# A hybrid decoder block on one core: sliding keys and latents projected ahead of the lower top-k searches, and a power seed for the reciprocal roots

## The chip, the cores and the metric

The kernel runs on one core of a Trainium2 chip. The metric is the device time of one execution in microseconds (us); times of stretches and instructions come from one profiled execution of the kernel before. The engines are named as the profile names them: PE (TensorE, matrix products, with its weight loads as PEld), DVE (VectorE), ACT (ScalarE), POOL (GpSimd) and SP (SyncE, which here only issues DMAs). Each engine works through its own queue of instructions in order.

## The reference

The program computes one layer of a decoder over 1024 tokens of width 1024, with 16 learned meta tokens ahead of them:

```
hn = rms_norm(h)                                  # h: 16 meta + 1024 tokens
aq, ak, av, bq, bkv, iq, ik, iw, gates = split(hn @ w_in)
o_a = sliding_window_attention(aq, ak, av)        # 8 heads, 2 key heads, window 128, sinks, bias
q_abs = rms_norm(bq) @ w_uq @ w_uk                # latents
c_kv  = rms_norm(bkv)
score = sum_h relu(iq_h . layer_norm(ik)) * iw_h  # indexer
sel   = top 256 admissible keys per query
o_b   = attention of q_abs over c_kv[sel] with bias, then w_uv
h = h + (sig(gate_a) * (o_a @ w_a) + sig(gate_b) * (o_b @ w_b)) @ w_out
h = h + SwiGLU(rms_norm(h))
out = rms_norm(h)
```

All is in float32. The kernel keeps that accuracy with matrix products of three terms: each operand is split into a high and a low part (`hi` and `lo`), and hi x hi, hi x lo and lo x hi are added up.

## The kernel before

The code is one program in four phases, `phase1`, `phase_b`, `phase_mix` and `phase_ffn`. Tokens lie in eight blocks of 128 (and the 16 meta tokens, block `NB`). A framework with a scheduler of its own puts the instructions of each engine into a queue, mostly by when their operands are due. `tc.issue_after(ins)` binds what is written inside it to stand behind `ins` on the engine of `ins`. Tiles of a pool with one name take turns in its buffers; a new tile waits until the readers of the old one are done.

The start of phase 1 is `norm_x` (L398): in two halves of four blocks it takes the sum of squares of each token (L413 on ACT, L415 on DVE), forms the reciprocal root with `rsqrt` (L213), scales the tokens (L424, L422), transposes them on PE (L429) and splits the result into high and low parts (L129 on ACT, L135 on DVE). The meta tokens are one column of the first half's sums. `rsqrt` is written for DVE: a seed from the bits of the number (L219, L220) and three Newton steps of three operations each. It is called for the two halves (`rx`), for the layer norm of the index keys (`rk`) and for the latents (`rlat`). The index weights `wi` are loaded, cast on ACT (L392) and given their low part on POOL (L393).

After the indexer has made the scores, `select_topk` (L780) finds the threshold of each query by bisection on 16 upper and then 16 lower bits. Seven rows of blocks are shared out: three go to DVE (`search_dve`, L829, whose counts are L838), and ACT has two groups (`search_act`, L864, whose counts are L880), one of 1040 and 400 and one of 784 and 528 columns. Each round of an ACT group is two counts on ACT and then four small steps on POOL (L887 to L890) that form the next threshold. Between the upper and the lower half stands `low_halves` (L819), a pass on POOL (L824) and one on DVE (L825) for each row. After the last round come the merge of both halves (L911 to L916), the counts L804 and the finishing of the masks (L811 to L815), all on DVE.

Beside the search run the projections. `proj_tokens` (L562) makes values and raw latents and ends with 17 scalings of `lraw` by `rlat` (L593). `window_inputs` (L664) projects the keys and queries of the sliding attention; `latents` (L596) transposes the scaled latents on PE (L198) into the two `tp` banks of PSUM and splits each into `qn` and `ck` (L129 on ACT, L135 on DVE); `sparse_inputs` (L629) multiplies these with the latent weights and stores queries, keys and values for phase B. Before, they are written in this order: `proj_tokens`, the lower search, `window_inputs` (keys, then queries), `latents`, `sparse_inputs`. The lower search of DVE is bound behind the last scaling L593 of the latents; ACT's are bound to nothing.

Then the window blocks follow: `bt_a` (the bias) is loaded and masked on POOL (L547, L548), keys `ka` and queries `qlo` are split (L707, L719), scores are made on PE and reduced on DVE (L739). Gates are projected in pieces that are put behind given matmuls of the other work.

`phase_mix` ends with the out-projection, added to `h` (L1242) block by block. For each block `row_scale` (L1259) forms the reciprocal root of the sum of squares (L1264), with two seed steps (L1266, L1267) and three Newton steps of two operations (L1269, L1270), all on DVE with one column. ACT scales the block (`xs`, L1279), PE transposes it (L1288) and DVE takes it out (`hb`, L1291). At the very end `final` (L1525) does the same once more for each block: ACT scales (L1533) and POOL multiplies with the gain (L1534), or DVE does both (L1536).

## Time and profile before

| | |
|---|---|
| median of 3 runs | 1484.69 us (1483.06 to 1485.52) |
| profiled execution | 1482.89 us, of which its span 1480.7 us |
| mean granted TensorE clock | 0.977 of full speed |
| PE busy | 1380.9 us (93%) |
| DVE busy | 1002.8 us (68%) |
| ACT busy | 817.0 us (55%) |
| POOL busy | 609.9 us (41%) |

The span is the time from the first to the last instruction. Shares of busy time are averages over stages that are limited by different engines; what one stage is worth is read in that stage. A row of the trace gives the start, the time, the engine, the line, the operation with the tile written and those read, the shape and the count; in square brackets stands the idle time of the engine ahead of it and what ended that. Durations of neighbouring instructions on one engine overlap a little, since an engine begins one before the last has drained; the step from start to start is the time that one holds the queue.

### The profile page before, as it was taken

What the parts mean: (1) busy time and instruction counts of PE and PEld (TensorE: products, weight loads), DVE (VectorE), ACT (ScalarE), POOL (GpSimd) and SP (SyncE); (2) the same over time, 40 slices, a digit from 0 to 9 for tenths busy, and PEclk for the clock granted to TensorE, in tenths of its full rate; (3) what the DMA queues carried; (4) which work ended last, traced back from release to release, by engine and by line L of the source; (5) the groups of instructions that cost most, each with busy time, mean ns of one, the idle gap of its engine ahead of it and who ended that gap; (6) DMA issues with size and microseconds to landing.
All of it is one profiled execution on the core that took longest, in us unless ns stands there. A gap on an engine that the chain in (4) does not pass through costs nothing.

```text
span 1480.7 us, 21298 instructions
## 1 busy us (share of the span) xinstructions
PE 1380.9 (93%) x6847; PEld 1149.3 (78%) x6847; DVE 1002.8 (68%) x2136; ACT 817.0 (55%) x1743; POOL 609.9 (41%) x873
## 2 busy tenths in 40 slices
PE   4999997698998899999899699999999999999997
PEld 3988985586776788888677578888888888888886
DVE  6258979556786796785797984445544547696585
ACT  5347977883896686785246633333333334444473
POOL 4135574446675556664200025554554554000004
PEclk9999999799999899999999899999999999999999
DMA  6421221256336555327912033332322338823332
GB/s 204 144 65 46 57 85 64 69 185 198 100 108 170 147 165 162 118 94 251 307 50 97 18 114 114 115 114 97 109 87 100 107 107 309 309 100 107 120 101 114
DMA packets 148038, 189.79 MB, mean 128 GB/s; under 512 B 11331, under 2 KB 95126, under 8 KB 147670
## 3 DMA queue, kind: packets, MB, share of 16 engines
q1 hardware_dynamic: 147568, 188.28, 39.3%
q8 instruction: 54, 0.88, 0.2%
q14 instruction: 58, 0.48, 0.1%
q0 software_dynamic: 160, 0.01, 0.0%
q10 hardware_dynamic: 198, 0.14, 0.0%
HBM read 133.49 MB, written 58.03 MB: 129 GB/s over the span
## 4 chain that ended last, share of the span: by engine, by line
PE 69%; DVE 14%; DMA 5%; issue 4%; ACT 3%; POOL 3%; SPq 1%; POOLq 0%; DVEq 0%; ACTq 0%
PE ps L193 28%; PE s L193 25%; PE gps L193 9%; DVE mask L838 3%; PE pv L1073 2%; DMA kraw<-bk_dram 1%; PE s L1031 1%; PE tp L1062 1%; PE tp L198 1%; POOL y L1534 1%; DVE ptl L133 1%; DVE pb L1035 1%; PE pv L193 1%; DMA ga<-gate_dram 1%; DVE hb L1291 1%
## 5 line engine op out<-in xcount | busy, mean ns | idle before, releaser
L1384 POOL TENSOR_TENSOR fhl<-fr,fhl 128x512 fp32r<-128x512 f32 x60 | 96.8, 1633 | 224.0 <-ACT fhl L1383 224.0
L1384 POOL TENSOR_TENSOR fhl<-fs,fhl 128x512 fp32r<-128x512 f32 x80 | 106.4, 1353 | 106.6 <-ACT fhl L1383 106.6
L193 PE MATMUL s<-ht,fhl 128*128 128x512 f32 x384 | 121.7, 393 | 0.7 <-ACT fhl L1383 0.4
L188 POOL TENSOR_TENSOR w_lo<-w_raw,w_hi 128x512 fp32r<-128x512 f32 x60 | 80.5, 1343 | 83.5 <-ACT w_hi L187 74.2
L193 PE MATMUL ps<-ht,fhl 128*128 128x512 f32 x320 | 101.1, 392 | 0.0
L193 PE MATMUL gps<-oh,w_hi 128*128 128x512 f32 x232 | 93.8, 404 | 4.5 <-ACT gt L938 4.3
L193 PE MATMUL gps<-ol,w_hi 128*128 128x512 f32 x232 | 92.0, 397 | 0.0
L193 PE MATMUL gps<-oh,w_lo 128*128 128x512 f32 x232 | 91.6, 395 | 0.0
L193 PE MATMUL s<-yhl,fhl 128*128 128x512 f32 x396 | 90.6, 389 | 0.0
L193 PE MATMUL ps<-yhl,fhl 128*128 128x512 f32 x396 | 90.3, 389 | 0.0
L1454 ACT CAST yhl<-wd 128x512 fp32r<-128x512 f32 x66 | 41.1, 622 | 88.1 <-PE ps L193 48.5
L193 PE MATMUL s<-h,fhl 128*128 128x512 f32 x272 | 87.6, 393 | 1.1 <-DVE hb L1291 1.1
L193 PE MATMUL ps<-h,fhl 128*128 128x512 f32 x256 | 82.9, 395 | 5.1 <-ACT h L1341 5.1
L133 DVE TENSOR_TENSOR ptl<-tp,pth 128x512 fp32r<-128x512 f32 (+2 forms) x112 | 70.6, 645 | 24.2 <-ACT pth L127 23.8
L193 PEld LDWEIGHTS s<-yhl,fhl 128*128 128x128 f32 x396 | 74.3, 188 | 15.5
L193 PEld LDWEIGHTS ps<-yhl,fhl 128*128 128x128 f32 x396 | 74.3, 188 | 15.5
L193 PEld LDWEIGHTS s<-ht,fhl 128*128 128x128 f32 x384 | 72.0, 188 | 18.4 <-ACT fhl L1383 1.3
L880 ACT ACTIVATE mask<-high,smallg 128x1040 bf16<-128x1040 int16 (+3 forms) x66 | 70.7, 1071 | 24.0 <-DVE high L825 13.3
L1383 ACT CAST fhl<-fr 128x512 fp32r<-128x512 f32 x66 | 39.8, 619 | 76.3 <-issue 36.1
L1455 DVE TENSOR_TENSOR yhl<-wd,yhl 128x512 fp32r<-128x512 f32 x66 | 45.5, 689 | 49.0 <-ACT yhl L1454 49.0
L193 PE MATMUL s<-lt,fhl 128*128 128x512 f32 x192 | 75.1, 392 | 0.0
L1383 ACT CAST fhl<-fs 128x512 fp32r<-128x512 f32 x88 | 54.6, 625 | 33.1 <-PE s L193 17.4
(496 smaller groups left out, 4203.0 us busy)
## 6 DMA issues: line engine op xcount, KB each, us to landing
fr<-in_w_ffn_gate SPq DMA_DIRECT2D x22, 512.0 KB, 4.0
fr<-in_w_ffn_up SPq DMA_DIRECT2D x22, 512.0 KB, 4.6
wd<-in_w_ffn_down SPq DMA_DIRECT2D x44, 256.0 KB, 5.0
da<-acts SPq DMA_DIRECT2D x44, 256.0 KB, 3.5
w_raw<-in_w_in SPq DMA_DIRECT2D x40, 256.0 KB, 3.1
act<-a SPq DMA_DIRECT2D x33, 256.0 KB, 2.1
da<-act SPq DMA_DIRECT2D x33, 256.0 KB, 3.9
acts<-s SPq DMA_DIRECT2D x33, 256.0 KB, 2.0
```

The source lines that it names most:

```text
L133: nc.vector.tensor_sub(lo, ps, hi.bitcast(F32))
L188: (nc.vector if lo_dve else nc.gpsimd).tensor_sub(t[1], t[2], t[0].bitcast(F32))
L193: mm = self.nc.tensor.matmul(*args, **kw)
L198: mm = self.nc.tensor.transpose(*args)
L838: nc.vector.tensor_scalar(self.mask[j], src[j], at[:, i:i + 1], None, op0=op, op1=ALU.add, accum_out=out[:, i:i + 1])
L880: nc.scalar.activation(self.mask[j], src[j], AF.Sign, bias=at[:, i:i + 1], scale=scale, accum_out=out[:, i:i + 1])
L1031: nc.tensor.matmul(ps[:, :n], q[k][:, h, qc:qc + P], kb[:, h, at:at + n], start=k == 0, stop=k == 1)
L1073: mm = nc.tensor.matmul(acc[:, e, :], v, t[k][:, 256 * i:256 * i + 256], start=r + i + k == 0, stop=False)
L1383: nc.scalar.copy(hi, a[name])
L1384: (nc.gpsimd if q else nc.vector).tensor_sub(lo, a[name], hi.bitcast(F32))
L1454: nc.scalar.copy(hi, src)
L1455: nc.vector.tensor_sub(lo, src, hi.bitcast(F32))
```

## The change

There are five parts. (1) The sliding keys become a function of their own, `window_keys`, and the order is now `proj_tokens`, `window_keys`, `latents`, the lower searches, `window_inputs` (queries alone), `sparse_inputs`. (2) `split` returns its two instructions, and every lower search is bound behind the last latent split: DVE's behind its DVE part, ACT's behind its ACT part. (3) The meta tokens have a sum and a root of their own (`ssm`, `rxm`). (4) The seed of every reciprocal root is one POOL operation, `pow` with a constant of -0.5, followed by one Newton step; `rsqrt` has then three DVE operations where it had eleven, and `row_scale` three (with its sum) where it had nine. (5) For the last block, `final` multiplies the second half row with the gain on POOL before the scale is there; then DVE scales the first half and ACT the second.

```diff
-    def rsqrt(self, pool, v, n, tag, e=0):
+    def rsqrt(self, pool, v, n, tag):
...
-        yi = y.bitcast(I32)
-        nc.vector.tensor_scalar(yi, v.bitcast(I32), 1, None, op0=ALU.logical_shift_right)
-        nc.vector.tensor_scalar(yi, yi, -1.0, float(0x5F3759DF + (e << 23)), op0=ALU.mult, op1=ALU.add)
-        for _ in range(3):
-            nc.vector.tensor_mul(a, y, y)
-            nc.vector.scalar_tensor_tensor(a, a, -0.5 / 4 ** e, v, op0=ALU.mult, op1=ALU.mult)
-            nc.vector.scalar_tensor_tensor(y, a, 1.5, y, op0=ALU.add, op1=ALU.mult)
+        nc.gpsimd.tensor_tensor(y, v, self.power[:, :n], op=ALU.pow)
+        nc.vector.tensor_mul(a, y, y)
+        nc.vector.scalar_tensor_tensor(a, a, -0.5, v, op0=ALU.mult, op1=ALU.mult)
+        nc.vector.scalar_tensor_tensor(y, a, 1.5, y, op0=ALU.add, op1=ALU.mult)
         return y
...
+        self.power = const.tile([P, 2 * NB + 2], F32, name="power")
+        nc.gpsimd.memset(self.power, -0.5)
...
             self.proj_tokens(lp)
+            self.window_keys(lp)
+            self.latents(lp)
             next(search, None)
             self.window_inputs(lp)
-            self.latents(lp)
             self.sparse_inputs(lp)
...
-            blocks = list(range(4 * half, 4 * half + 4)) + ([NB] if half == 0 else [])
+            blocks = list(range(4 * half, 4 * half + 4))
...
+                m = tiles[NB]
+                sm = xp.tile([P, 1], F32, name="ssm")
+                nc.vector.memset(sm, 1.0)
+                nc.scalar.activation(junk[0][:NM, :], m, AF.Square, accum_out=sm[:NM])
+                nc.vector.tensor_scalar(sm, sm, 1.0 / D, EPS, op0=ALU.mult, op1=ALU.add)
+                nc.vector.tensor_scalar(m, m, self.rsqrt(xp, sm, 1, "rxm")[:NM], None, op0=ALU.mult)
...
-                self.split(pt[:, :n * len(bs)], *[t[:, at:at + n * len(bs)] for t in dst], scale=scales[c])
+                self.scaled_act, self.scaled = self.split(pt[:, :n * len(bs)], *[t[:, at:at + n * len(bs)] for t in dst], scale=scales[c])
...
-        with self.tc.issue_after(self.scaled):
-            next(searches[-1])
+        for s in searches:
+            with self.tc.issue_after(self.scaled if s is searches[-1] else self.scaled_act):
+                next(s)
...
-        yi = y.bitcast(I32)
-        nc.vector.tensor_scalar(yi, v.bitcast(I32), 1, None, op0=ALU.logical_shift_right)
-        nc.vector.tensor_scalar(yi, yi, -1.0, float(0x5F3759DF), op0=ALU.mult, op1=ALU.add)
-        for s in (1, 2, 16):
-            nc.vector.scalar_tensor_tensor(z, y, y, v, op0=ALU.mult, op1=ALU.mult)
-            self.scaled_dve = nc.vector.scalar_tensor_tensor(y, z, -3.0 * s * s, y, op0=ALU.add, op1=ALU.mult).ins
+        nc.gpsimd.tensor_tensor(y, v, self.power[:, :1], op=ALU.pow)
+        nc.vector.scalar_tensor_tensor(z, y, y, v, op0=ALU.mult, op1=ALU.mult)
+        self.scaled_dve = nc.vector.scalar_tensor_tensor(y, z, -3.0, y, op0=ALU.add, op1=ALU.mult).ins
...
+                        if t == NB - 1 and nh == 1:
+                            nc.gpsimd.tensor_mul(outs[t][:, 512:], self.h1[:, t, 512:], gain[:, 512:])
...
+        if b == NB - 1:
+            nc.vector.scalar_tensor_tensor(y[:, :512], self.h1[:, b, :512], r, gain[:, :512], op0=ALU.mult, op1=ALU.mult)
+            nc.scalar.activation(y[:, 512:], y[:, 512:], AF.Copy, scale=r)
+            for nh in range(2):
+                nc.sync.dma_start(self.out[0, P * b:P * b + P, 512 * nh:512 * nh + 512], y[:, 512 * nh:512 * nh + 512])
+            return
```

The constants with which the gains are multiplied follow the other scale of `row_scale` (-1/256 becomes -16). Lines of the changed kernel are numbered by its own file: 7 or 8 more than before in phase 1 (L593 becomes L600, L845 becomes L856, L739 becomes L749).

Three places of the order. On DVE, around the latent splits (L135, written to `ck` and `qn`), before: they stand behind the last step of the lower search (L861), its counts (L804) and between the first mask operations (L811, L812).

```order
L861 SCALAR_TENSOR_TENSOR small<-smalld,small 128x3
L804 TENSOR_SCALAR mask_145,small<-sc_203,small 128x272
L804 TENSOR_SCALAR mask_148,small<-sc_203,small 128x656
L804 TENSOR_SCALAR mask_150,small<-sc_202,small 128x912
L811 TENSOR_SCALAR mask_145<-sc_203,small 128x272
L135 SCALAR_TENSOR_TENSOR ck_2826<-tp,vec,ck_2825 128x16
L811 TENSOR_SCALAR mask_148<-sc_203,small 128x656
L135 SCALAR_TENSOR_TENSOR qn_2828<-tp,vec,qn_2827 128x512
L811 TENSOR_SCALAR mask_150<-sc_202,small 128x912
```

The same splits in the changed kernel, on DVE, right behind the last scaling of the latents (now L600):

```order
L600 TENSOR_SCALAR lraw<-lraw,rlat_y 128x128
L135 SCALAR_TENSOR_TENSOR ck_2127<-tp,vec,ck_2126 128x16
L135 SCALAR_TENSOR_TENSOR qn_2129<-tp,vec,qn_2128 128x512 x2
L135 SCALAR_TENSOR_TENSOR ck_2127<-tp,vec,ck_2126 128x512
L135 SCALAR_TENSOR_TENSOR qn_2129<-tp,vec,qn_2128 128x512 x2
L135 SCALAR_TENSOR_TENSOR ck_2127<-tp,vec,ck_2126 128x512
L856 TENSOR_SCALAR smalld<-small 128x3
L849 TENSOR_SCALAR mask_150,smalld<-high,small 128x912
```

All seven have moved ahead of the lower search, which begins with L856.

On DVE at the first scores of the window blocks, before (L815 is the last mask operation, L707, L719 and L695 split keys, queries and values, L739 reduces a score):

```order
L815 TENSOR_SCALAR mask_151<-mask_151 128x1040
L707 TENSOR_TENSOR ka_3140<-kraw,ka_3140 64x1040
L719 TENSOR_TENSOR qlo_3161<-qraw,qhi 64x1024
L695 TENSOR_TENSOR va<-kraw,va 16x2x64
L695 TENSOR_TENSOR va<-kraw,va 128x16x64
L739 ISA pa,nma<-s,bt_a,nsink 128x144
L739 ISA nma 128x1
```

And in the changed kernel, on DVE, where L815 is the count that was L804 and L749 the score that was L739:

```order
L815 TENSOR_SCALAR mask_147,small<-sc_202,small 128x528
L815 TENSOR_SCALAR mask_149,small<-sc_203,small 128x784
L749 ISA pa,nma<-s,bt_a,nsink 128x144
L749 ISA nma 128x1
L822 TENSOR_SCALAR mask_146<-sc_203,small 128x400
L749 ISA pa,nma<-s,bt_a,nsink 128x144
L749 ISA nma 128x1
L822 TENSOR_SCALAR mask_151<-sc_202,small 128x1040
L705 TENSOR_TENSOR va<-kraw,va 128x16x64
L822 TENSOR_SCALAR mask_147<-sc_202,small 128x528
```

The scores have moved ahead of the mask finishing of ACT's four rows (L822 was L811), which now stands between them and those that follow.

On POOL at the two passes over the bias (L547, L548), before, where L541 finishes the causal part of a mask:

```order
L541 AFFINE_SELECT mask_147<-mask_147 128x128
L541 AFFINE_SELECT mask_148<-mask_148 128x128
L541 AFFINE_SELECT mask_149<-mask_149 128x128
L939 TENSOR_SCALAR gt<-gt 128x512
L547 AFFINE_SELECT bt_a<-bt_a 128x2048
L541 AFFINE_SELECT mask_150<-mask_150 128x128
L188 TENSOR_TENSOR w_lo<-w_raw,w_hi 128x512
L548 AFFINE_SELECT bt_a<-bt_a 128x2048
```

They stand there among the finished masks. In the changed kernel, on POOL at the end of the searches (L899 to L901 are the steps of a round, before L888 to L890; L554 and L555 are the two passes over the bias, before L547 and L548):

```order
L898 TENSOR_SCALAR smallg_1209<-smallg_1209 128x2
L554 AFFINE_SELECT bt_a<-bt_a 128x2048
L899 TENSOR_TENSOR smallg_1195<-smallg_1195 128x2
L555 AFFINE_SELECT bt_a<-bt_a 128x2048
L899 TENSOR_TENSOR smallg_1209<-smallg_1209 128x2
L900 TENSOR_SCALAR smallg_1195<-smallg_1195 128x2
```

Both passes have moved ahead of the last rounds' steps, where before they stood behind the end of both searches.

## Rows read from the trace of the kernel before

**Rows 1.** From the page: busy time, share of the span and instructions of each engine, and the share of each engine in the chain of work that ended last.

```profile
PE 1380.9 (93%) x6847; PEld 1149.3 (78%) x6847; DVE 1002.8 (68%) x2136; ACT 817.0 (55%) x1743; POOL 609.9 (41%) x873
...
PE 69%; DVE 14%; DMA 5%; issue 4%; ACT 3%; POOL 3%; SPq 1%; POOLq 0%; DVEq 0%; ACTq 0%
```

**Rows 2.** The table of stretches: start and end, length, busy time of PE, PEld, DVE, ACT and POOL with their counts, then the granted clock of PE, the DMA share and the rate in GB/s.

```profile
0.00:40.00 40.00, 19.58 (x111) 16.23 (x112) 28.71 (x65) 24.29 (x43) 17.98 (x34) 1.00 0.64 201
40.00:190.00 150.00, 148.43 (x965) 134.60 (x964) 95.19 (x221) 96.50 (x249) 59.89 (x134) 1.00 0.27 76
...
250.00:270.00 20.00, 0.80 (x1) 0.29 (x1) 19.20 (x57) 16.53 (x40) 11.25 (x40) 0.56 0.16 53
270.00:320.00 50.00, 48.41 (x216) 39.86 (x217) 16.18 (x25) 44.97 (x100) 23.58 (x73) 0.94 0.36 119
...
800.00:835.00 35.00, 22.73 (x118) 18.75 (x117) 30.64 (x88) 19.63 (x34) 0.00 (x0) 0.80 0.15 61
...
860.00:1440.00 580.00, 579.96 (x2534) 475.31 (x2534) 343.83 (x460) 228.33 (x413) 204.54 (x141) 1.00 0.39 133
```

**Rows 3.** The timeline at the largest hole of PE: start, time, engine, line, operation, tiles, shape and count, then the idle time ahead and its releaser. First two rows of PE, then three of DVE.

```profile
248.58 0.39 PE L193 MATMUL gps<-oh,w_lo 128*128 128x512 f32 x1
...
270.02 2.25 PE L198 MATMUL tp<-ident,lraw 128*128 128x128 f32 x8 [6.86 <-DVE ck L135]
...
203.58 0.17 DVE L845 TENSOR_SCALAR smalld<-small 128x3 f32<-128x3 int32 x1
...
267.14 0.49 DVE L804 TENSOR_SCALAR_CACHE_REDUCE mask<-sc,small 128x272 bf16<-128x272 f32 x1
...
269.74 0.23 DVE L135 SCALAR_TENSOR_TENSOR ck<-tp,vec,ck 128x16 fp32r<-128x16 f32 x1
```

**Rows 4.** The timeline of the stretch 200 to 225: the first matmuls of the queries on PE, the pass over DVE's three rows on POOL, and rounds of the two groups on ACT.

```profile
201.18 0.62 PE L193 MATMUL s<-xt,wa_hi 128*128 128x512 f32 x2
201.65 0.40 PE L193 MATMUL s<-xt,wa_lo 128*128 128x512 f32 x1
...
206.25 5.43 POOL L824 TENSOR_SCALAR mask<-sc,smalld 128x912 uint16<-128x912 uint16 x3 [0.44 <-DVE smalld L846]
...
219.21 1.15 ACT L880 ACTIVATE mask<-high,smallg 128x1040 bf16<-128x1040 int16 x1
...
220.97 0.94 ACT L880 ACTIVATE mask<-high,smallg 128x784 bf16<-128x784 uint16 x1
...
222.62 1.15 ACT L880 ACTIVATE mask<-high,smallg 128x1040 bf16<-128x1040 int16 x1
```

**Rows 5.** The timeline from the end of the search to the scores of the window blocks: the first row of the merge on DVE, the first mask operation behind the last counts, the split of `ka`, the first score and the second pair of block 1; then the first pass over `bt_a` on POOL and the issue of its DMA by SP.

```profile
320.49 0.17 DVE L913 TENSOR_SCALAR smallg<-smallg 128x2 int32<-128x2 f32 x1 [15.10 <-POOL smallg L888]
...
323.80 0.42 DVE L811 TENSOR_SCALAR mask<-sc,small 128x400 bf16<-128x400 f32 x1
...
348.35 2.22 DVE L707 TENSOR_TENSOR ka<-kraw,ka 64x1040 fp32r<-64x1040 f32 x1
...
357.68 0.36 DVE L739 CUSTOM_DVE_ANT_0 pa<-s,bt_a,nsink 128x144 f32<-128x144 f32 x1
...
372.22 0.48 DVE L739 CUSTOM_DVE_ANT_0 pa<-s,bt_a,nsink 128x256 f32<-128x256 f32 x1 [3.25 <-PE s L193]
...
344.80 2.97 POOL L547 TENSOR_SCALAR_AFFINE_SELECT bt_a<-bt_a 128x2048 f32<-128x2048 f32 x1 [0.29 <-DMA bt_a<-bias_dram]
...
335.97 0.37 SPq L300 DMA_DIRECT2D bt_a<-bias_dram  x1
```

**Rows 6.** Elementwise work of two inputs on POOL and DVE. First two groups of the page, with busy time, mean ns of one and idle time ahead; then the view of one line of POOL, with shortest, median and longest time of one in ns and the starts of the first and the last.

```profile
L188 POOL TENSOR_TENSOR w_lo<-w_raw,w_hi 128x512 fp32r<-128x512 f32 x60 | 80.5, 1343 | 83.5 <-ACT w_hi L187 74.2
...
L133 DVE TENSOR_TENSOR ptl<-tp,pth 128x512 fp32r<-128x512 f32 (+2 forms) x112 | 70.6, 645 | 24.2 <-ACT pth L127 23.8
...
L888 POOL TENSOR_TENSOR smallg<-smallg x64: 187/194/1983, 127.1 to 320.3; 128x2 f32<-128x2 f32 x64
```

**Rows 7.** The timeline of the start: POOL's subtraction for the first index weight, the scaling of half 0, the last step of half 1's root on DVE, and the cast of an index weight on ACT.

```profile
11.78 0.87 POOL L393 TENSOR_TENSOR wi<-wa_raw,wi 128x324 fp32r<-128x324 f32 x1 [6.45 <-ACT wi L392]
...
16.92 2.73 DVE L424 TENSOR_SCALAR x<-x,rx_y 128x1024 f32<-128x1024 f32 x4
...
32.30 0.15 DVE L224 SCALAR_TENSOR_TENSOR rx_y<-rx_a,rx_y 128x5 f32<-128x5 f32 x1
...
34.12 0.45 ACT L392 CAST wi<-wa_raw 128x324 fp32r<-128x324 f32 x1
```

**Rows 8.** The timeline ahead of the FFN: the last addition to `h`, two of the steps of `row_scale` on DVE, and ACT's scaling of the blocks.

```profile
812.33 0.68 DVE L1242 TENSOR_TENSOR h<-h,ps 128x512 f32<-128x512 f32 x1
...
822.52 0.20 DVE L1269 SCALAR_TENSOR_TENSOR rh<-rh 128x1 f32<-128x1 f32 x1
822.65 0.15 DVE L1270 SCALAR_TENSOR_TENSOR rh<-rh 128x1 f32<-128x1 f32 x1
...
824.22 2.19 ACT L1279 ACTIVATE xs<-h,rh 128x1024 f32<-128x1024 f32 x2 [4.34 <-DVE rh L1270]
```

**Rows 9.** The timeline of the end: the sum of the last block's root on DVE, ACT's scaling and POOL's multiplication with the gain.

```profile
1473.37 0.21 DVE L1264 TENSOR_SCALAR rh<-ss 128x1 f32<-128x1 f32 x1 [0.85 <-ACT sq L1256]
...
1475.39 0.72 ACT L1533 ACTIVATE y<-h,rh 128x512 f32<-128x512 f32 x1 [2.05 <-issue]
...
1476.19 1.26 POOL L1534 TENSOR_TENSOR y<-y,gain 128x512 f32<-128x512 f32 x1 [5.60 <-ACT y L1533]
```

More of the change, by code (lines that the diff above doesn't have):

```diff
@@ L401, in norm_x @@
         tiles = self.xtiles
-        st = [xp.tile([P, 5], F32, name=f"ss{h}") for h in range(2)]
+        st = [xp.tile([P, 4], F32, name=f"ss{h}") for h in range(2)]
         for h in range(2):
@@ L657, in window_inputs, with window_keys @@
     def window_inputs(self, lp):
+        for g in range(2):
+            w = self.weights(self.wp, raw_pool=self.wg, src=self.win(256 * g, 256), **WA)
+            for h in range(2):
+                for m in range(2):
+                    ps = self.bank()
+                    self.feature_cols(ps, w, slice(P * m, P * m + P), NM + 512 * h, 512)
+                    self.stored(lp, ps, self.wq_dram[2 * g + m][h], 0.125)
+    def window_keys(self, lp):
         w = self.weights(self.wp, raw_pool=self.wg, src=self.win(512, 128), **WA)
@@ L665, in window_inputs @@
             at += n
-        for g in range(2):
-            w = self.weights(self.wp, raw_pool=self.wg, src=self.win(256 * g, 256), **WA)
-            for h in range(2):
-                for m in range(2):
-                    ps = self.bank()
-                    self.feature_cols(ps, w, slice(P * m, P * m + P), NM + 512 * h, 512)
-                    self.stored(lp, ps, self.wq_dram[2 * g + m][h], 0.125)
     def doubled(self, dst, src):
```

23 lines of the change are left out of this document (13 added, 10 removed).

## The prediction

> **What bounds the kernel now.** I read the page's busy shares and its chain first. TensorE (PE) is busy for 1380.9 of 1480.7 us and makes 69% of the chain; VectorE (DVE) adds 14% [rows 1]. So an edit pays only where PE stands still, or runs at the lower of its two clock levels. The table of stretches says where that is [rows 2]: idle PE is the stretch less its busy time, and of the 99.8 us in all, 20.4 lie before 40 us, 19.2 in 250 to 270 and 12.3 in 800 to 835. From 860 to 1440 PE is full, so what is gained ahead of it stays gained.
>
> The largest hole is read on two engines [rows 3]. PE ends a run of matmuls at 248.58 + 0.39 and goes on at 270.02, with transposes of `lraw` that were released by DVE's low part of a latent split (`ck`, L135). That split is 0.23 us long, at 269.74. What stood ahead of it in DVE's queue is the lower-half search, begun at 203.58, and the counts L804 that follow it from 267.14. The splits free the two `tp` banks that the transposes share, so PE waited behind 64 us of search that no matmul needs. The granted clock fell to 0.56 in 250 to 270 and was 0.94 in 270 to 320 [rows 2]: 0.06 x 50 = 3 us more.
>
> **Latents ahead of the lower search.** After the change DVE's queue has all seven latent splits ahead of L856, which opens the lower search; before, they stood behind L804. When does the last one come? PE starts the queries at 201.18, and the third matmul follows at 201.65, so 0.23 each [rows 4]. The last four transposes stand behind 77 of them and 17 other transposes: 201.2 + 18 + 2 to 3 = about 222, and with the split 223. So the search starts 20 us later than at 203.58. It lasts 63.6 us (267.14 - 203.58), giving 287, and its rows' counts and scans follow until about 300. DVE is busy 16.2 of 50 us in 270 to 320 [rows 2], so this has room. PE's hole then goes: 19.2 + 3 = 22 us are the most that this edit can return.
>
> **What is late next.** ScalarE (ACT) now holds back its searches too. The group of 784 and 528 elements was in its lower rounds at 220.97; it must now wait for the last split and then for the `low_halves` work on GpSimd (POOL), of which DVE's three rows alone take 5.43 us [rows 4]. With the four other rows at some 5 more, and the last upper count ahead, I get 236 for its first lower round. From there 16 rounds of both groups, 1.76 and 1.65 us each (219.21 to 220.97 to 222.62, [rows 4]), are 54.6 us. In the new order 49 copies and casts stand between them, at an estimated 0.5 each by their widths: 25. That is 316 with no gap, against 320.49 before, when the merge began [rows 5]. So the search ends hardly earlier although PE does.
>
> POOL adds to it: the two passes over `bt_a` (2.97 us each) now stand ahead of the last rounds' L899, and they wait for a DMA which was issued at 335.97 and released POOL at 344.80 [rows 5]. It follows the last store of the sparse inputs; with PE 19 us earlier it is issued at 317, lands at 326, and the second pass ends near 332. Then come the merge and two counts (320.49 to 323.80) and two counts more: the first window score (L749) at about 338 instead of 357.68.
>
> That alone would be 20 us. But before, the mask finishing (323.80 to 348.35, 24.5 us with some clears) was over by then [rows 5]; now it lies between the first scores on DVE, with 4 us of counts and scans of the second group. Up to the second pair of block 1 I count 22.5 us of it, 3.4 for L717 and the `va` part and 1.6 for four scores: 338 + 27.5 = 365.5, where that pair stood at 372.22. So the sure gain is 7 us and the most is 22. The scores after it keep their order, so a shift is kept. I take 9, near the lower end because the walk gives that, and a little more because some mask work falls into waits that DVE has anyway (3.25 ahead of that pair). Range 0 to 22.
>
> **The square root on POOL.** No row of before shows `pow`. The nearest are POOL's small operations, median 0.19 us on 128x2; at the far end stands a subtraction on 128x512, 1.34 [rows 6]. I take 0.3 with the hand-over, as the small rows are nearest to 128x1 and 128x4, and keep 0.2 to 1.3 (below nothing is excluded, since it adds work to POOL).
>
> *Start*: the chain for half 0 ends with the scaling at 16.92. After, its sum no longer waits for the meta square; `pow` can start when POOL's subtraction ends (11.78 + 0.87 = 12.65), three DVE operations of 0.2 follow, and the scaling comes at about 13.7. Half 1 has its scale at 32.30 + 0.15, eleven operations stretched by splits between them; with three it could be 24 to 25. But PE's full stretch from 40 us also needs the last index weights, whose cast is at 34.12 on a loop of load, cast and subtraction that moves only by 2 to 3.5 us, by the 3.2 of half 0 [rows 7]. I take 2.5, range 0 to 6. PE is busy 148.4 of the next 150 us [rows 2], so it is kept.
>
> *Ahead of the FFN*: DVE has the last `h` at 812.33, and ACT's `xs` at 824.22 had waited 4.34 us for the last scale L1270 [rows 8]. Between the two DVE runs 24 steps on 128x1 that go, 0.13 us or less from start to start (822.52 to 822.65), and four `hb` operations of 0.6 that now stand ahead of the last `h`: 24 x 0.1 + 2.4 = 4.8, less 0.3 for one uncovered `pow`. I take 4.5, range 1 to 7. POOL has nothing else to do there (0.00 busy in 800 to 835 [rows 2]).
>
> *End*: L1264 at 1473.37 to ACT's `y` at 1475.39 is 2.0 us in nine steps; six go (1.35), a `pow` comes (0.3). POOL's multiplication of 1.26 behind ACT's `y` [rows 9] is done early, on half a row that does not need the scale. 1.35 - 0.3 + 1.3 = 2.3; I take 2, range 1 to 2.6. The constants and memsets cost nothing that PE waits for, and the chain `rk` sits under full PE in 40 to 190.
>
> **A rule against it.** POOL's subtraction of 128x512 takes 1343 ns and DVE's 645 (a few narrower ones among them) [rows 6]. By the Trainium skill, GPSIMD Engine Reference (4.1 Engine selection), elementwise work belongs on VectorE, since GPSIMD needs about twice as long for two inputs; on that width this trace agrees. If it held for 128x1, each `pow` would cost 0.2 more and the sum be 1 to 2 us less; POOL's 0.19 on 128x2 stands beside DVE's 0.15 to 0.20 on 128x1 [rows 6, 8], so I leave it out.
>
> **Sum.** 2.5 + 9 + 4.5 + 2 = 18 us. The profiled execution took 1482.89 (span 1480.7 and 2.2 around it), which gives 1464.9. It lies 1.8 below the median of the runs, 1484.69, so I predict 1466.7, or 1467.
>
> **Rivals.**
> 1. *The whole hole comes back.* Mask work falls into waits, and block 1 follows the first score: the middle gives 22 instead of 9. For it: DVE waited 3.25 us there before [rows 5]. Against: 22 us of mask work in one in-order queue. 1467 - 13 = 1454. Chance 0.18.
> 2. *The gain is handed to the search.* ACT has no slack from 236 on, and POOL's weight subtractions of 1.34 stand between its handshakes; each can add its length. With seven uncovered the search ends 9 us later and the middle gives nothing: 1476. Against: two groups take turns, and one's round covers the other's handshake. Chance 0.23.
> 3. *Slower: `pow` is long.* Eight calls lie one behind another on the path: two at the start, one ahead of the latents, four queued ahead of the FFN, and the last. At t us each the change loses 8 (t - 0.3); from t = 2.6 on the 18 us are gone. At 4 us: 1467 + 30 = 1497. For it: nothing shows its time, and even 128x2 rows reach 1.98. Against: their median is 0.19 [rows 6]. Chance 0.09.
> 4. *Only the first `pow` is long.* If it takes the whole of the chain it replaces (16.92 - 12.65 = 4.3 us), half 0 gains nothing, nor do the index weights: the start term is 0 and the time 1469 to 1470. Chance 0.06. By the Trainium skill, GPSIMD Engine Reference (2.1 Instruction dispatch), a freshly loaded routine costs approximately 6 us at its first call, which would cost some 2 us more; no run here shows it.
>
> **How the numbers follow.** My own case has 0.40 and goes from 1459 to 1473 by its terms; 0.04 are left for what I don't see. 1453 to 1481 leaves out rival 3, part of rival 1 and a search that ends far later: about 2 in 10. A measurement of this kernel can tell about 0.2%, 3 us, from no change. Faster than 1481.7: my case, rivals 1 and 4, and nearly all of rival 2, 0.82. Slower than 1487.7: rival 3, and 0.03 for a search that ends past 345, 0.12. Between: 0.06.
>
> **What would show it.** Right: PE busy throughout 250 to 270 with no fall of the clock there; the lower search on DVE from about 223 to 287; the first lower round of the 784 group near 236; the last near 316 to 330; the first L749 near 338 with mask work between the scores; `pow` rows under 0.5 us; the `xs` transposes 4 to 5 us sooner after the last `h`. Wrong: a new PE hole of over 20 us at 310 to 345; `pow` above 1 us; scores no earlier than 355.

## The result and the profile after

The changed kernel takes 1468.94 us (median of 5 runs, 1465.71 to 1471.66), beside 1485.03 for the kernel before on the same chip: a ratio of 0.9886, with a 95% interval from 0.9873 to 0.9899. The ratios here and below are taken over the runs of both kernels, so they differ a little from the quotients of the medians. The forecast was 1467. The profiled execution of after has a span of 1467.3 us, 13.4 less than before; that of before (1482.89) lies 1 to 4 us under the medians measured beside the runs below, so differences against its trace come out that much too small. Lines of the changed kernel's phase 1 stand up to 11 further down than before, not 7 or 8 alone (L845 became L856, L739 became L749).

The page of after, busy time and shares of the chain, answers to [rows 1]:

```profile
PE 1384.1 (94%) x6847; PEld 1153.8 (79%) x6847; DVE 993.3 (68%) x2013; ACT 817.1 (56%) x1743; POOL 630.3 (43%) x895
...
PE 70%; DVE 11%; DMA 5%; ACT 5%; issue 4%; POOL 3%; SPq 1%; POOLq 0%; ACTq 0%; DVEq 0%
```

The stretches of after, with the columns of [rows 2] (start and end, length, busy PE, PEld, DVE, ACT, POOL, then PE's granted clock, DMA share, GB/s):

```profile
0.00:40.00 40.00, 22.21 (x122) 17.64 (x123) 27.95 (x57) 24.59 (x43) 20.08 (x38) 0.96 0.62 189
...
250.00:270.00 20.00, 17.02 (x77) 13.54 (x76) 19.10 (x57) 20.00 (x48) 10.14 (x36) 1.00 0.40 141
270.00:320.00 50.00, 47.90 (x204) 38.27 (x204) 32.47 (x77) 45.78 (x102) 30.51 (x79) 0.97 0.58 180
320.00:370.00 50.00, 35.40 (x141) 27.84 (x141) 47.86 (x92) 19.17 (x49) 27.59 (x39) 0.80 0.39 111
...
800.00:835.00 35.00, 24.75 (x110) 19.97 (x109) 33.80 (x66) 25.26 (x47) 4.67 (x4) 0.80 0.15 61
```

The old hole is filled: PE is busy 17.02 us in 250 to 270, not 0.80, at full clock. A new one is in 320 to 370: 14.6 us idle at a mean clock of 0.80, with DVE busy 47.86 of 50. Before, PE was idle 6.4 us there, at 0.99:

```profile
320.00:370.00 50.00, 43.61 (x193) 34.40 (x192) 37.93 (x61) 21.38 (x43) 28.99 (x31) 0.99 0.66 200
```

DVE's timeline of after there answers to [rows 3, 5]: the last latent split, the counts of ACT's rows, then the first score, the second pair of block 0, block 1's second pair and the window's last score.

```profile
224.89 0.75 DVE L135 SCALAR_TENSOR_TENSOR ck<-tp,vec,ck 128x512 fp32r<-128x512 f32 x1 [3.18 <-ACT ck L129]
...
324.60 0.62 DVE L815 TENSOR_SCALAR_CACHE_REDUCE mask<-sc,small 128x400 bf16<-128x400 f32 x1
...
328.00 0.36 DVE L749 CUSTOM_DVE_ANT_0 pa<-s,bt_a,nsink 128x144 f32<-128x144 f32 x1
...
344.47 0.35 DVE L749 CUSTOM_DVE_ANT_0 pa<-s,bt_a,nsink 128x144 f32<-128x144 f32 x1
...
359.79 0.47 DVE L749 CUSTOM_DVE_ANT_0 pa<-s,bt_a,nsink 128x256 f32<-128x256 f32 x1
...
441.50 0.48 DVE L749 CUSTOM_DVE_ANT_0 pa<-s,bt_a,nsink 128x256 f32<-128x256 f32 x1
```

The end of the search did not pass its gain on. The hand-over, from ACT's last count to the last row of the merge on DVE, took 1.8 us before (320.18 to 321.99) and takes 10.7 in after (313.95 to 324.68), so the counts behind it begin 2.6 us later than before (324.60 for 322.02) though ACT ends 6.2 earlier. In between stand POOL's last steps, its two passes over `bt_a` and splits of the window on DVE. ACT's last count, the merge's last row and the window's last score, before:

```profile
319.96 0.22 ACT L880 ACTIVATION_READ_ACCUMULATOR mask<-sc,smallg 128x1 f32 x1
...
321.82 0.16 DVE L916 TENSOR_TENSOR small<-smallg 128x2 int32<-128x2 int32 x1
...
449.43 0.48 DVE L739 CUSTOM_DVE_ANT_0 pa<-s,bt_a,nsink 128x256 f32<-128x256 f32 x1
```

The first two in after:

```profile
313.76 0.19 ACT L891 ACTIVATION_READ_ACCUMULATOR mask<-sc,smallg 128x1 f32 x1
...
324.02 0.65 DVE L927 TENSOR_TENSOR small<-smallg 128x2 int32<-128x2 int32 x2
```

PE's timeline has the other side, waits of 4.42 and 6.00 us for these reductions:

```profile
344.89 0.58 PE L194 MATMUL s<-ka,qhi 128*128 128x256 f32 x1 [4.42 <-DVE nma L749]
...
357.28 0.58 PE L194 MATMUL s<-ka,qhi 128*128 128x256 f32 x1 [6.00 <-DVE nma L749]
```

The roots on POOL, which no row of before showed, by number of columns: the first on 4, then 9, 18, the longest on 1 (ahead of the FFN) and the last one of the run on 1.

```profile
12.44 1.05 POOL L219 TENSOR_TENSOR rx_y<-ss,power 128x4 f32<-128x4 f32 x1
...
82.12 1.80 POOL L219 TENSOR_TENSOR rk_y<-var,power 128x9 f32<-128x9 f32 x1 [14.55 <-DVE var L503]
...
194.81 3.24 POOL L219 TENSOR_TENSOR rlat_y<-ssq,power 128x18 f32<-128x18 f32 x1
...
808.85 1.96 POOL L1276 TENSOR_TENSOR rh<-rh,power 128x1 f32<-128x1 f32 x1
...
1461.67 0.55 POOL L1276 TENSOR_TENSOR rh<-rh,power 128x1 f32<-128x1 f32 x1 [4.50 <-DVE rh L1275]
```

Ahead of the FFN, where [rows 8] stood, the scaling on ACT and the first FFN score on PE:

```profile
811.74 2.18 ACT L1287 ACTIVATE xs<-h,rh 128x1024 f32<-128x1024 f32 x2
...
820.12 0.50 PE L194 MATMUL s<-h,fhl 128*128 128x512 f32 x1 [0.54 <-DVE hb L1299]
```

The same milestones of every run, read from its timeline (us; "pv" is the start of the last value product of phase B, "mix" that of the last matmul of the out-projection):

| run | last latent split ends | first score | window's last score ends | pv | mix | first FFN score | last `h` | span |
|---|---|---|---|---|---|---|---|---|
| before | 291.9 | 357.7 | 449.9 | 686.4 | 811.2 | 832.9 | 1471.8 | 1480.7 |
| after | 225.6 | 328.0 | 442.0 | 679.4 | 805.0 | 820.1 | 1459.8 | 1467.3 |
| e1_old_order | 288.1 | 355.1 | 447.4 | 685.5 | 810.6 | 825.8 | 1467.3 | 1474.8 |
| e2_order_alone | 222.2 | 331.4 | 442.7 | 677.8 | 801.0 | 822.1 | 1463.7 | 1472.6 |
| e3_act_free | 234.8 | 339.3 | 432.4 | 669.2 | 795.0 | 810.1 | 1449.8 | 1457.2 |
| e4_mask_late | 225.7 | 323.3 | 447.1 | 680.7 | 805.6 | 820.8 | 1461.2 | 1468.7 |
| e5_row_dve | 224.4 | 328.0 | 441.8 | 679.4 | 803.5 | 824.6 | 1464.5 | 1473.1 |
| e6_rlat_dve | 222.8 | 330.2 | 438.0 | 672.6 | 798.1 | 813.3 | 1454.2 | 1461.6 |
| e7_bt_behind | 227.9 | 335.2 | 441.9 | 680.0 | 805.4 | 820.6 | 1461.1 | 1468.6 |
| e8_spread | 228.2 | 326.1 | 444.9 | 681.2 | 806.1 | 821.2 | 1462.1 | 1469.5 |
| f1_free_rlat | 235.1 | 343.9 | 436.2 | 669.9 | 793.4 | 808.6 | 1449.5 | 1457.0 |
| f4_free_rlat_pool | 234.2 | 339.7 | 436.6 | 670.3 | 795.2 | 810.3 | 1451.1 | 1458.6 |
| x2_free_masks_held | 234.2 | 336.2 | 433.1 | 670.7 | 797.4 | 812.5 | 1453.8 | 1461.2 |
| x1_no_ties | 226.0 | 328.7 | 427.0 | 663.9 | 789.1 | 804.3 | 1445.6 | 1453.0 |

### The profile page after: what moved, and what is told of

Read it like the earlier page. It is cut to its first block, busy times and chain, and to the rows that moved or that the text cites. A ratio compares the mean times of both kernels' runs of the same rounds, so it can differ in the third digit from the quotient of the medians.

```text
span 1467.3 us, 21211 instructions
## 1 busy us (share of the span) xinstructions
PE 1384.1 (94%) x6847; PEld 1153.8 (79%) x6847; DVE 993.3 (68%) x2013; ACT 817.1 (56%) x1743; POOL 630.3 (43%) x895
## 4 chain that ended last, share of the span: by engine, by line
PE 70%; DVE 11%; DMA 5%; ACT 5%; issue 4%; POOL 3%; SPq 1%; POOLq 0%; ACTq 0%; DVEq 0%
PE ps L194 29%; PE s L194 24%; PE gps L194 9%; PE pv L1084 2%; PE s L1042 2%; ACT mask L891 2%; PE tp L1073 1%; DMA kraw<-bk_dram 1%; PE tp L199 1%; DMA ga<-gate_dram 1%; PE pv L194 1%; DVE pb L1046 1%; DVE wd L1493 1%; POOL mask L835 1%; DMA da<-act 1%
## 5 line engine op out<-in xcount | busy, mean ns | idle before, releaser
L891 ACT ACTIVATE mask<-high,smallg 128x1040 bf16<-128x1040 uint16 (+2 forms) x66 | 71.2, 1079 | 11.4 <-DVE high L836 5.4
```

The source lines that it names most:

```text
L891: nc.scalar.activation(self.mask[j], src[j], AF.Sign, bias=at[:, i:i + 1], scale=scale, accum_out=out[:, i:i + 1])
```

## The experiments

**The two halves apart.** `e1_old_order` is the changed kernel with the old order, `e2_order_alone` the kernel before with the new order and its holds.

```diff
# e1_old_order, against after
-            self.window_keys(lp)
-            self.latents(lp)
             next(search, None)
+            self.window_keys(lp)
             self.window_inputs(lp)
+            self.latents(lp)
             self.sparse_inputs(lp)
...
-        for s in searches:
-            with self.tc.issue_after(self.scaled if s is searches[-1] else self.scaled_act):
-                next(s)
+        with self.tc.issue_after(self.scaled):
+            next(searches[-1])
```

> The changed kernel with its roots, meta norm and final normalisation kept, and the old order put back: the search resumed first, then keys, queries, latents; only VectorE's lower half is held behind the latent scaling. Theory (the order is worth about 5 us at the end, the rest comes from the roots): the hole in TensorE's queue near 250 to 270 us is back, the first matmuls of the run still come some 3 us earlier than before, the last h to the end still takes about 7.5 us; 1474 us (1472 to 1477; a little more if the root of 18 columns on POOL, 3.2 us, now stands on the way to the latents). Rival A (the new hole at 340 to 368 us takes all of the order's gain back): 1469, as the changed kernel. Rival B (the order carries the whole gain): 1483 or more.

Measured: 1475.97 us against 1486.5, ratio 0.992 (0.9901 to 0.9939). The hole is back: PE is busy 3.07 of 20 us in 250 to 270.

> The kernel before with the order keys, latents, search, queries and the two holds alone; roots, meta norm and final constants as before. Theory: about 5 us better than before, 1480 (1477 to 1482); first score reductions some 30 us earlier than before, last h to the end unchanged at about 8.9 us, first FFN scores as late behind the last h as before. Rival A: 1485, no gain. Rival B (order carries it all): 1470.

Measured: 1474.6 us against 1486.5, ratio 0.9923 (0.9906 to 0.994). So each half alone is worth some 0.8%, and 1.57% together if they added up; the change gives 1.14%. The order alone is worth twice what I expected (11.9 us by the medians, for 5), and about 0.4%, 6 us, goes lost where the two meet. With old roots the run has no early start, yet its latent splits end at 222.2 and not at 225.6, and pv comes at 677.8 and not 679.4. The scalings ahead of the splits say why; DVE's first one in the run with the order alone and in after (one row joins 17 and 15 of them):

```profile
198.03 6.20 DVE L595 TENSOR_SCALAR lraw<-lraw,rlat_y 16x128 f32<-16x128 f32 x17
```

```profile
192.52 0.95 DVE L594 TENSOR_SCALAR ssq<-ssq 128x9 f32<-128x9 f32 x1 [8.11 <-ACT junk L587]
...
198.08 0.18 DVE L220 TENSOR_TENSOR rlat_a<-rlat_y 128x18 f32<-128x18 f32 x1 [4.62 <-POOL rlat_y L219]
...
200.99 4.61 DVE L600 TENSOR_SCALAR lraw<-lraw,rlat_y 16x128 f32<-16x128 f32 x15
```

DVE waits 4.62 us for the root of 18 columns, and the early start is spent there.

**That root back on DVE** (`e6_rlat_dve`).

```diff
-        nc.gpsimd.tensor_tensor(y, v, self.power[:, :n], op=ALU.pow)
+        if n < 18:
+            nc.gpsimd.tensor_tensor(y, v, self.power[:, :n], op=ALU.pow)
...
+        else:
...
+            for _ in range(3):
```

> The changed kernel with one root, that of 18 columns ahead of the latents, back on VectorE (11 passes); all other roots stay on POOL. Theory: this root is what makes the two halves of the change add up to less than their sum: with it on POOL the scalings start at 200.99 us though the run is 3 us ahead; on VectorE they start near 197.1, the last latent split ends at 219 to 222 instead of 225.6, the lower halves and the masks come as much earlier, phase B's last matmul comes 3 to 4.5 us earlier than 679.4, and the time is 1464 to 1466. Rival (the search's end is set by ScalarE's counting rounds and the mask work on VectorE, not by when the splits end): 1467.5 to 1470.

Measured: 1463.31 us against 1484.08, ratio 0.9854 (0.9833 to 0.9874): 0.3% below the change, with intervals that only touch. The trace agrees: the splits end 2.9 us earlier, the window's last score comes 4.0 earlier, pv 6.8. On DVE the eleven passes take 3.6 us; its first and last row, and the first scaling:

```profile
193.45 1.31 DVE L226 TENSOR_SCALAR rlat_y<-ssq 128x18 int32<-128x18 int32 x1
...
196.72 0.18 DVE L231 SCALAR_TENSOR_TENSOR rlat_y<-rlat_a,rlat_y 128x18 f32<-128x18 f32 x1
197.00 6.20 DVE L609 TENSOR_SCALAR lraw<-lraw,rlat_y 16x128 f32<-16x128 f32 x17
```

With POOL the way from the sum to the scaling was 200.99 - 193.5 = 7.5 us, and less than half of that is the root: it began 1.3 us after the sum, behind a subtraction on POOL, took 3.24, and the three passes that follow took 2.9 us, two of them 1.35 and 1.22 beside more subtractions on POOL, where such a pass takes 0.18 here. So one of the five kinds of root should have stayed where it was.

**The roots of single columns** (`e5_row_dve`: `row_scale` with its old seed and three Newton rounds on DVE, its constants with it).

```diff
-        nc.gpsimd.tensor_tensor(y, v, self.power[:, :1], op=ALU.pow)
...
+        for s in (1, 2, 16):
```

> The changed kernel with the old row_scale on VectorE (two seed passes and three Newton rounds, the constants -1/256 back); rsqrt's roots stay on POOL and the order stays. My reading: this part alone carries what is won ahead of the FFN and at the end. From the run with the order alone, the first FFN scores follow the mix's last matmul by 21.1 us instead of 15.2 (plus 5.9), the tail from the last h is 8.9 instead of 7.5 (plus 1.4), and the mix is 2 us shorter without the hand-overs to POOL (123.2 against 125.6): 1469 + 5.3 = 1474 (1472 to 1476). Rival: the gap ahead of the FFN closed for another reason (the earlier arrival, the split of meta's norm): 1468 to 1470.

Measured: 1475.58 us against 1484.08, ratio 0.9934 (0.9917 to 0.9951). From mix to the first FFN score it is 21.1 us, as in before (21.7), against 15.2 with POOL; from the last `h` to the end 8.6 against 7.5. In the stage ahead of mix it is 1.4 us shorter without POOL. So this part is worth its 6 + 1 - 1.4.

**ScalarE's searches without their hold** (`e3_act_free`).

```diff
-        for s in searches:
-            with self.tc.issue_after(self.scaled if s is searches[-1] else self.scaled_act):
-                next(s)
+        with self.tc.issue_after(self.scaled):
+            next(searches[-1])
```

> The changed kernel without the hold on ScalarE's lower-half searches (VectorE's hold stays). Rival to my reading, that this hold delays the searches and with them the masks and first scores: the last ScalarE counting round ends some 5 us before 313 us and the time falls to 1464 to 1467. My theory: the searches' counting rounds then stand ahead of the latents' high copies on ScalarE, the splits end later than 224.9 us, TensorE's hole between 250 and 270 is partly back, and in this build's instruction order 28 more VectorE instructions stand ahead of the first score reduction; 1470 to 1476.

Measured: 1459.96 us against 1486.5, ratio 0.9825 (0.9806 to 0.9844). My reading fell, and the rival's direction came, by more than it said: ACT's last count ends at 309.48, 4.5 us earlier than in after, and the time is under its 1464. The counting rounds do stand ahead of the latents' copies (the splits end at 234.8, 9 us later), but PE is still busy 17.98 us in 250 to 270, with 78 matmuls for 77: nothing needs the splits that early. What it wins is on DVE, the stretches after 270 and two of the mask counts:

```profile
270.00:320.00 50.00, 46.33 (x207) 37.68 (x206) 48.44 (x115) 38.06 (x82) 30.84 (x66) 1.00 0.56 181
320.00:370.00 50.00, 43.04 (x189) 32.86 (x189) 42.93 (x85) 25.83 (x67) 32.14 (x35) 0.90 0.40 119
```

```profile
303.75 0.76 DVE L814 TENSOR_SCALAR_CACHE_REDUCE mask<-sc,small 128x528 bf16<-128x528 f32 x1
...
314.61 0.63 DVE L814 TENSOR_SCALAR_CACHE_REDUCE mask<-sc,small 128x400 bf16<-128x400 f32 x1
```

The two groups no longer end together: the counts of one begin at 303.75, of the other at 314.61, where after has all four from 324.60. The last merge ends at 314.58, 10.1 us earlier than in after: 4.5 of it is ACT's, 5.6 the hand-over, which takes 5.1 us and not 10.7. DVE does 48.44 us of work in 270 to 320 instead of 32.47, and the first score, which comes 11 us later, does not hurt: the window's last one comes 9.6 earlier.

**Whether the mask work or its place counts.** `e4_mask_late` holds counting and finishing of the masks behind block 1's scores; `e8_spread` puts row block j's behind window block j; `x1_no_ties` leaves out the ranking of ties.

```diff
# e4_mask_late; e8_spread has a yield and such a hold in every j
+        yield
+        with self.tc.issue_after(self.reduced):
             for j in range(1, NB):
...
# x1_no_ties
+            if j not in DVE_ROWS:
+                nc.vector.tensor_scalar(eq[:, :W], s, t, None, op0=ALU.is_ge)
...
+                continue
```

> The changed kernel with the counting and finishing of the top-k masks on VectorE held behind the score reductions of the second block of the sliding window. Theory (the mask work between the first score reductions makes the new hole at 340 to 368 us, and VectorE has 24 us of idle time in 370 to 460): the second pair of block 0 follows the first within 2 us instead of 16, block 1's second pair is reduced near 340 to 345 us instead of 359.8, TensorE is busy 6 to 12 us more in 320 to 370, the window stage ends that much earlier than 454.7 and the time is 1459 to 1464. Rival (VectorE bounds the whole stage, the same work only stands between later blocks): TensorE waits for reductions behind block 1 instead, and the time stays at 1467 to 1471.

Measured: 1470.96 us against 1486.5, ratio 0.9898 (0.9881 to 0.9915). The rival came. Blocks 0 and 1 are quick (block 1's second pair at 336.54), and then PE stands in one piece:

```profile
359.50 0.58 PE L194 MATMUL s<-ka,qhi 128*128 128x256 f32 x1 [10.75 <-DVE nma L751]
```

> The changed kernel with the counting and finishing of each row block's top-k mask on VectorE held behind the score reductions of the sliding window's block of the same number, so that seven pieces of 1 to 7 us stand between blocks instead of all in one place. The run with all of it behind block 1 moved TensorE's wait (10.75 us in one piece at 359.5) and won nothing. Theory A (what counts is VectorE's work between the end of the searches and the last score reduction, wherever it stands): window stage ends within 3 us of 442.0, time 1466 to 1471. Theory B (the size of the single piece counts: TensorE has block b+1's transposes and products to run meanwhile, and VectorE has 24 us idle in 370 to 460): window stage ends 6 to 10 us earlier, time 1459 to 1464.

Measured: 1469.23 us against 1484.08, ratio 0.9883 (0.9858 to 0.9909); the window's last score ends at 444.9, 2.9 later than in after. Theory A holds: small pieces win no more than one large one.

> The changed kernel without the ranking of ties in the masks of ScalarE's four row blocks (every score at or above the threshold is let in); it leaves out some 16 us of VectorE's work between 324 and 362 us (equality passes 4.7, scans 6.7, compares about 4). Theory (VectorE's mask work between the searches' end and the window's last score sets the window stage): last window score 10 to 15 us earlier than 442.0, time 1454 to 1460. Rival (TensorE's own matmuls in this stage set its end, the waits only move): last window score within 3 us, time 1466 to 1470.

Measured: 1454.57 us against 1484.09, ratio 0.9798 (0.9778 to 0.9819). Some 16 us less of DVE's work give 14.4 us, and all of it by the window's last score (15.0 earlier). PE's two stretches in this run:

```profile
270.00:320.00 50.00, 47.92 (x205) 38.35 (x204) 32.08 (x77) 46.10 (x104) 29.91 (x79) 0.97 0.58 183
320.00:370.00 50.00, 46.51 (x226) 36.16 (x225) 43.91 (x117) 31.99 (x85) 36.48 (x51) 1.00 0.50 137
```

PE's hole of 320 to 370 is nearly gone (46.51 busy, 35.40 in after) and its clock is full. From 324 to the window's last score DVE is busy 101.92 of 118 us in after and 85.93 of 103 here:

```profile
324.00:442.00 118.00, 100.32 (x505) 82.16 (x504) 101.92 (x267) 78.37 (x221) 72.16 (x99) 0.91 0.37 106
```

```profile
324.00:427.00 103.00, 96.63 (x508) 78.11 (x507) 85.93 (x255) 78.68 (x221) 71.93 (x99) 1.00 0.44 123
```

So from the end of the searches to the window's last score it is the amount of DVE's work that sets the time, and not at which of the three places tried it stands. How far this goes is open: here PE is busy 96.63 of the 103 us already.

**Which mask work.** `x2_free_masks_held` is the run without ScalarE's hold, with the counts, equality passes and scans of the group that ends first held behind the last merge.

```diff
+        late = lambda j: self.tc.issue_after(self.merged[ACT_ROWS[0]]) if j in ACT_ROWS[1] else nullcontext()
         for j in range(1, NB):
-            nc.vector.tensor_scalar(self.mask[j], self.scores[j], col(thr, j), None, op0=ALU.is_gt, op1=ALU.add, accum_out=col(cnt, j))
+            with late(j):
+                nc.vector.tensor_scalar(self.mask[j], self.scores[j], col(thr, j), None, op0=ALU.is_gt, op1=ALU.add, accum_out=col(cnt, j))
```

> The run without ScalarE's hold, but with the first-ended group's counts, equality passes and scans (303.75 to 309.18 us there, 5.4 us of VectorE, which then had nothing else to do) held behind the last group's merge at 314.5. Theory (what that run won is mask work done while VectorE was idle): about 5 us of the 9 are lost, last window score 436 to 438 instead of 432.4, time 1463 to 1466. Rival (what it won is only that the last merge comes at 314.6 instead of 324.6; the first group's masks matter little): last window score within 2 us of 432.4, time 1459 to 1461.5.

Measured: 1457.65 us against 1485.88, ratio 0.9806 (0.9793 to 0.982), the window's last score at 433.1 against 432.4. The rival came by the last score (its time, 1459 to 1461.5, was undercut; the profiled execution, 1462.98, is the longest of the five), but the run is not clean:

```profile
309.92 0.76 DVE L817 TENSOR_SCALAR_CACHE_REDUCE mask<-sc,small 128x528 bf16<-128x528 f32 x1
...
312.10 1.29 DVE L817 TENSOR_SCALAR_CACHE_REDUCE mask<-sc,small 128x1040 bf16<-128x1040 f32 x1
```

With the 5.4 us out of the way the last merge itself ended at 310.0, 4.6 us earlier than at 314.6, so that as much was won ahead of it as was put behind it. What is shown is that the point where the last merge ends and the work left behind it count together; how much of the 9 us belongs to either is open.

**POOL's two passes over the bias table** (`e7_bt_behind`).

```diff
-        self.window_masks()
+        with self.tc.issue_after(self.searched):
+            self.window_masks()
```

> The changed kernel with the two selects over the bias table (2 us each, POOL) held behind POOL's last operation of the searches. Theory: these passes and what they delay put 9.0 us between ScalarE's last count (313.9) and the last merge (322.8), in the run without ScalarE's hold it is 3.1; held behind, the last merge ends near 317, the masks finish up to 6 us earlier and the time is 1463 to 1466. Rival: the first score reductions need the table, which is ready 4 us after the merge, and the scheduler puts the mask work of 10 us ahead of them instead, so that the time stays within 2 us of 1469 or rises.

Measured: 1470.13 us against 1484.08, ratio 0.989 (0.9869 to 0.9911), no change. POOL was done with the searches at 317.65 instead of 322.8, but the scheduler set the six passes of the merge (on 128x2) one by one between mask and split work on DVE, and they ended at 330.66, later than the 324.67 of after. Rows of POOL, then of DVE:

```profile
317.46 0.19 POOL L921 TENSOR_TENSOR smallg<-smallg 128x2 f32<-128x2 f32 x1
...
317.60 1.95 POOL L554 TENSOR_SCALAR_AFFINE_SELECT bt_a<-bt_a 128x2048 f32<-128x2048 f32 x1
...
324.34 4.92 POOL L555 TENSOR_SCALAR_AFFINE_SELECT bt_a<-bt_a 128x2048 f32<-128x2048 f32 x1
...
329.24 1.40 POOL L189 TENSOR_TENSOR w_lo<-w_raw,w_hi 128x512 fp32r<-128x512 f32 x1
...
318.20 1.38 DVE L925 TENSOR_SCALAR smallg<-smallg 128x2 int32<-128x2 f32 x1
...
327.44 1.84 DVE L927 TENSOR_SCALAR smallg<-smallg 128x2 int32<-128x2 int32 x1
...
329.40 1.26 DVE L928 TENSOR_TENSOR small<-smallg 128x2 int32<-128x2 int32 x1
```

The hand-over grew from 10.7 to 14.4 us (316.24 to 330.66). So what the passes cost in after stays open; this way of moving them costs as much as it gives.

**Both gains together.** `f1_free_rlat` joins the edits of `e3_act_free` and `e6_rlat_dve`; `f4_free_rlat_pool` gives the masks' last scaling to POOL as well (`nc.vector` becomes `nc.gpsimd` in that line).

> The changed kernel without the hold on ScalarE's searches and with the root of 18 columns on VectorE: the two edits that each made it faster (1460.0 and 1463.3), together. If they act at different places (one starts the latents earlier, the other ends the first group of the searches earlier so that its masks are made while VectorE was idle), 1454 to 1457. If both do no more than bring the same mask work forward into the same idle time, 1459 to 1461.

Measured: 1460.32 us against 1484.09, ratio 0.984 (0.982 to 0.9859), no better than `e3_act_free`. The latent splits end at 235.1, as there (234.8): with the hold gone ACT's counting rounds stand ahead of the copies, and an earlier root finds no one waiting.

> The same with the masks' last scaling pass (seven passes, 3.6 us on VectorE in the changed kernel) on POOL, which also has the causal select behind it. If VectorE's work in this stage is still the bound: 2 to 4 us less than the run without it. Rival (POOL, which also multiplies the softmax rows that TensorE's transposes wait for, becomes late; or TensorE is the bound by now): no better, up to 3 us worse.

Measured: 1461.54 us against 1484.09, ratio 0.9849 (0.9831 to 0.9868), as the rival had it. POOL's scalings and selects were long beside DVE's work (3.76 and 4.13 us on 272 and 128 columns, at 331.94 and 335.77), and PE waited 7.07 us at 343.14 for a low half of a weight that POOL makes.

## Why the prediction came out right, and where it did not

The total is 2 us off, but by luck in part: the terms were wrong by more and made up for some of each other. Of the 18 us forecast the medians show 16.1, the traces of before and after 13.4. By the traces, term by term:

- *Start, taken at 2.5*: PE's first products with the index weights begin at 36.27 instead of 39.24, 3.0 us. The scaling of half 0 came at 14.98, not at 13.7: the first root took 1.05 us, and on DVE a pass for the meta tokens' own root (14.04, 0.82 us) stands ahead of its last step. Before, then after:

```profile
39.24 2.36 PE L193 MATMUL ps<-wi,xt 128*16 128x256 f32 x19
```

```profile
36.27 2.26 PE L194 MATMUL ps<-wi,xt 128*16 128x256 f32 x18
```

- *Middle, taken at 9*: 449.9 - 442.0 less the start's 3.0 is 4.9. The hole was filled as said: splits done at 225.6 (said: 223), lower search on DVE until 289.38 (287), last ACT round at 313.9 (316). The first score came 10 us earlier than I had it (328.00 for 338), because the passes over `bt_a` ran at 313.89 and 315.95 and not until 332; block 1's second pair at 359.79 (365.5) was 12.4 us earlier than in before. The step that failed is: "The scores after it keep their order, so a shift is kept". In PE's queue of the changed kernel 13, 11, 13 and 24 matmuls fewer stand ahead of the two pairs of key products of block 1 and of block 2 than in before. They run behind them, at 0.23 each [rows 4] 5.5 us for the 24. At block 5's first pair as many stand ahead as before, and there the 12.4 are down to 7.2 (380.62 for 387.79); at the window's end it is 7.9. What I should have summed is DVE's work up to the last score, as `x1_no_ties` shows. A part of the miss is not the order's: the order alone moves the window's end by 7.2 us (`e2_order_alone`) and the roots alone by 2.5 (`e1_old_order`), but both together by 7.9. The wide root of the next point stands in the way: with it back on DVE (`e6_rlat_dve`) it is 11.9.
- *One root of the middle, priced at 0.3 as all the others*: this is the term that was mis-sized most. I took the price of POOL's 128x2 rows, and it goes with the columns: 0.54 on 1 at the least, 1.05 on 4, 1.80 on 9, 3.24 on 18. Between the first and the last that is (3.24 - 0.54) / 17 = 0.16 a column, an estimate from these rows that gives 1.02 and 1.81 for the other two. It is not the width alone: the eight of one column ahead of the FFN took 0.54 to 1.96, beside DVE's work. `pow` above 1 us was one of the prediction's own signs of being wrong, and no root came in under its 0.5. The root of 18, "one ahead of the latents" in rival 3, makes DVE wait 4.62 us; putting it back on DVE gives 0.3%, about 5 us.
- *Ahead of the FFN, taken at 4.5*: from mix to the first FFN score 21.7 became 15.2, 6.5 us; `e5_row_dve` shows that 5.9 of it are this edit. The stage ahead of it gave back 1.7 (7.9 at the window's end, 6.2 at mix), of which 1.4 comes with the single roots on POOL by the same run; the FFN gave back another 0.7 (12.7 at its first score, 12.0 at the last `h`).
- *End, taken at 2*: 8.9 became 7.5, 1.4. Here `pow` took 0.55 and 0.66 with the hand-over, where I had 0.3.

Rival 1, the whole hole back, did not come: mask work did not fall into waits, it made them. Rival 2 fell as it stands: the search did not end 9 us later than its 316, it ended at 313.9. But the hand-over behind it took 10.7 us, where I had 16 (316 to 332, for the passes over `bt_a`), and the hold on ACT costs 0.6% by `e3_act_free`. I had walked through that hold and taken it as part of the change, without asking what the order would give without it. Rival 3 needed all roots past 2.6 us, and only one is. Rival 4 fell: the first root took 1.05 us, the second of the same shape 1.02, so the first call was not dear; the 6 us of the page cited there were not seen.

I left out a rule. By the Trainium skill, GPSIMD Engine Reference (4.1 Engine selection), GPSIMD is the slower place for elementwise work. No run here tests it on the same operation: a `pow` on POOL with two or three passes on DVE stands against eight or eleven passes on DVE. By that comparison DVE is the better place for 18 columns (3.6 us against 7.5) and POOL for one column (15.2 against 21.1 us from mix to the first FFN score, in `e5_row_dve`).

## What to carry to other kernels

Before filling a hole of the busiest engine, add up what the engine behind it must still do until the stage's last hand-over: here moving DVE's mask work behind later scores was worth nothing, leaving out 16 us of it 14.4. When a chain of small passes is moved to another engine, price it call by call, by its width, by what stands ahead of it in the other engine's queue and by its hand-over, and leave a dear one on the path where it is. A hold that protects an early step is worth a run without it: all four versions without ACT's hold (0.9806 to 0.9849) beat both kernels, and their intervals end below the one of the change.

## What the runs showed of the hardware that was not expected

DVE's small passes and POOL's large ones stretch each other. A pass over 128x2, 0.16 us when alone on DVE, stood for 1.2 to 1.84 us in `e7_bt_behind` while POOL ran its selects over the bias table or a weight's subtraction, and one select took 4.92 us where it takes 1.95 in after. The ends tell more than the times: each of these four passes ended within 0.03 us of the POOL row beside it (the one at 327.44 at 329.28, the select at 329.26), as if held until then, and the select ended 1.75 us after two long scans on DVE that began with it (until 327.51). In after such a row stands in the hand-over itself, the first of the merge beside the second select; POOL, then DVE:

```profile
315.95 1.95 POOL L555 TENSOR_SCALAR_AFFINE_SELECT bt_a<-bt_a 128x2048 f32<-128x2048 f32 x1
...
316.04 1.89 DVE L924 TENSOR_SCALAR smallg<-smallg 128x2 int32<-128x2 f32 x1 [6.47 <-POOL smallg L899]
```

By the Trainium skill, SBUF — State Buffer (Who interferes with whom), the two engines share a pair of ports which one instruction holds to its end, where DVE's instruction reads two inputs from SBUF while GpSimd reads there, or runs in a mode that uses both ports. These rows fit that; which mode a pass ran in no trace shows, and no run took it apart.
